# A dense expert table in another layout: 1152 column-major dense columns and 896 gathered ones, with the low parts shared between VectorE and GpSimd

## The chip, the cores and the metric

The kernel runs on one core of a Trainium2 chip. The metric is device time in microseconds from launch to end; lower is better. TensorE (PE in the profile), VectorE (DVE), ScalarE (ACT) and GpSimd (POOL) work side by side, each in the order in which its instructions were written; SyncE (SP) only issues DMAs, and GpSimd issues the indirect ones.

## What is computed

One decoder block on 256 tokens of width 2048: a mixing part (sparse attention and convolution), a layer norm that gives `y`, and then an expert-retrieval layer, which is where the change lies:

```python
q = (yb @ wq).reshape(bsz, PEER_BLOCK, PEER_HEADS, 2, PK_HALF)
...                                  # two top-16 lists per head, then the 16 best of 256 sums
eidx = jnp.take_along_axis(cidx, pos, axis=-1)
g = jax.nn.softmax(top.astype(jnp.float32), axis=-1)
u = u_tab[eidx]                      # u_tab: 16384 experts x 2048
v = v_tab[eidx]
h = jax.nn.gelu(jnp.einsum('btd,bthkd->bthk', yb, u))
return jnp.einsum('bthk,bthkd->btd', g * h, v).astype(y.dtype)
```

Each of the 256 tokens picks 16 experts in each of 8 heads, 128 experts in all, and needs the dot product of its own `y` with each picked row of `u_tab`. The numbers are float32, and matrix products are made exact enough by splitting each operand into a high and a low part and adding three products (high·high, high·low, low·high).

## The kernel before

The 2048 columns of `u_tab` are cut in two. For the first `UD` columns the products of **all** 16384 experts with all tokens are computed densely on TensorE. For the last `UG` columns only the picked rows are fetched, by indirect DMAs, and VectorE takes their dot products. A later stage picks the dense products of the chosen experts and adds the two.

The **dense stage** is the loop over `j` of 128 groups of 128 experts (`for j in range(P)` behind `later_steps`). Before the change a group is handled as two halves of 512 columns:

- `u_load` (SP) fetches 128 rows of 1024 columns into `ur`, `URB` groups ahead.
- `u_split` turns four blocks of 128x128 on TensorE into a PSUM tile `ut` (line 1235); ScalarE writes the high part `uh` from it (1238), VectorE the low part `ul` (1239).
- `u_mult` runs 12 matmuls of 128x256 for each half (`mm3`, lines 293 to 295), so 24 a group, summed in `hp`; `u_keep` (ScalarE, 1516) stores the sums in `W`.
- `dots_until` keeps the gathered side going. `gather` lets GpSimd issue one indirect DMA, one picked row for each of 128 tokens (1167); `dot` is VectorE's product and sum with the token's `y`, which lies in PSUM as `yp` (1178). There are 256 such gathers (2 token tiles of 128 picks). They go through a ring of `GBUFS` + `GMORE` = 5 buffers `gu`, so a gather waits on GpSimd until the dot that frees its buffer is done.
- `later_steps` gives VectorE a piece of the routing (top-16 search, expert numbers) in each round.

`LATE` gathers are left for the **lookup stage** behind the loop, which picks the dense products with small matmuls into `bank` tiles (1669, 1717); there a third of the products is done by GpSimd (`x_dot`, 1831) and summed by ScalarE (1841). A **value stage** with the second table follows (`f`, `gv`, `vr`, `vh`). Ahead of the loop the query product `pwq` runs, with low parts `lo` by GpSimd (254), and the first gathers and splits are mixed in. All orders are written out by hand; nothing is planned at run time.

Of the kernel before, what the change touches and what calls it, by code (L numbers as in the profile page):

```python
# [51 lines left out]
LATE = 52  # L52
# [8 lines left out]
UHB = 3  # L61
URB = 3
# [14 lines left out]
def tile_hybrid_block(  # L77
# [3 lines left out]
    w_out, ln1_g, ln1_b, wq, keys, u_tab, v_tab, ln2_g, ln2_b, out,  # L81
# [4 lines left out]
    u_tab, v_tab, out = u_tab[0], v_tab[0], out[0]  # L86
# [210 lines left out]
    def half_of(name, i):  # L297
        pool, n = ((slota, UK), (slots, KD - UK))[i]
        return flat3(pool.tile([P, n * T], F32R, name=f"{name}{n}", tag=f"t_{name[1]}"), n, T)

# [779 lines left out]
    def route_steps(h, tt, banked=False):  # L1080
# [32 lines left out]
        for s, dst in ((0, i1), (1, i2)):  # L1113
# [212 lines left out]
    def y_turn(cb, tt, low=True, tag="S"):  # L1326
        if yt[0][cb * 512 // UD] is None:
            yt[0][1], yt[1][1] = half_of("yh", 1), half_of("yl", 1)
# [5 lines left out]
        hs = chunks(yt[0], cb * 4, 4, ts)  # L1334
        nc.scalar.activation(hs, p3, AF.Copy)
        if low:
            nc.vector.tensor_tensor(chunks(yt[1], cb * 4, 4, ts), p3, hs.bitcast(F32), op=OP.subtract)
        else:
            return lambda: nc.vector.tensor_tensor(chunks(yt[1], cb * 4, 4, ts), p3, hs.bitcast(F32),
# [814 lines left out]
```

## Time and profile before

| what | value |
|---|---|
| time, median of 3 runs | 1638.65 us (1637.99 to 1642.5) |
| the profiled execution, its own time | 1637.97 us |
| its span, first to last instruction | 1636.2 us |
| TensorE busy | 1611.7 us, 99% of the span |
| VectorE busy | 1433.8 us, 88% |
| ScalarE, GpSimd busy | 811.0 us and 901.2 us |
| DMA | 475.19 MB, mean 290 GB/s |

Busy time is the time an engine had an instruction in work. Matmuls overlap each other, so the distance between the starts of two matmuls, and not their length, is what one costs. The DMA share is the mean busy share of the 16 DMA engines; GB/s is what they moved.

### The profile page before, as it was taken

How to read it: one execution, taken by the hardware profiler on the slowest of the kernel's cores; microseconds unless marked ns; L12 is line 12 of the kernel's file. 1: busy time of each engine (PE TensorE's matmuls, PEld its weight loads, DVE VectorE, ACT ScalarE, POOL GpSimd, SP SyncE). 2: the span in 40 equal slices, each digit the busy share in tenths (PEclk: the TensorE clock that was granted, in tenths of full speed). 3: DMA queues.
4: the chain of work that ended last, by engine and by line, in shares of the span. 5: the costliest groups of instructions: out<-in, count | busy, mean ns of one | idle time of the engine just before them, and what ended most of it. 6: DMA issues, size and time to landing. Idle time of an engine off the chain costs nothing.

```text
span 1636.2 us, 30621 instructions
## 1 busy us (share of the span) xinstructions
PE 1611.7 (99%) x11627; PEld 1495.9 (91%) x11627; DVE 1433.8 (88%) x2655; ACT 811.0 (50%) x1262; POOL 901.2 (55%) x661
## 2 busy tenths in 40 slices
PE   9999999999999999999999999999999999999997
PEld 9999999988999999999999997878888888888886
DVE  6999677756769999999999889988889999989998
ACT  5445766645434444444444445777444444444443
POOL 1886000065783333333333347757888887877883
PEclk9999999999999999999999999999999999999999
DMA  9774536365759999999999998776999999999997
GB/s 290 233 232 144 174 109 202 104 232 182 242 183 332 351 347 353 350 349 348 352 348 355 358 319 277 244 230 188 341 365 355 362 360 347 367 366 353 361 360 250
DMA packets 178348, 475.19 MB, mean 290 GB/s; under 512 B 18304, under 2 KB 86424, under 8 KB 177944
## 3 DMA queue, kind: packets, MB, share of 16 engines
q1 hardware_dynamic: 117188, 253.62, 45.7%
q0 software_dynamic: 57488, 218.66, 36.4%
q8 instruction: 91, 1.49, 0.4%
q10 hardware_dynamic: 3524, 0.95, 0.3%
q14 instruction: 57, 0.47, 0.1%
HBM read 468.32 MB, written 4.85 MB: 289 GB/s over the span
## 4 chain that ended last, share of the span: by engine, by line
PE 83%; DVE 7%; issue 3%; POOL 3%; ACT 2%; DMA 2%; POOLq 0%; DVEq 0%; ACTq 0%
PE f L294 9%; PE f L295 9%; PE f L293 9%; PE hp L295 7%; PE hp L293 7%; PE hp L294 6%; PE ut L1235 6%; PE bank L1717 2%; PE bank L1669 2%; DVE taps L487 2%; PE pwq L295 2%; PE pwq L294 2%; PE pwq L293 2%; DVE gu L1178 1%; PE mixa L293 1%
## 5 line engine op out<-in xcount | busy, mean ns | idle before, releaser
L1740 POOL DMA_INDIRECT gv<-in_peer_v_dram,e x256 | 396.6, 1549 | 98.1 <-DVE gacc L1745 52.5
L1167 POOL DMA_INDIRECT gu<-in_peer_u_dram,eu x206 | 193.2, 938 | 309.7 <-DVE gu L1178 219.3
L1780 ACT ACTIVATE vh<-vr 128x1408 fp32r<-128x1408 f32 (+1 forms) x129 | 175.7, 1364 | 275.0 <-DVE gacc L1745 233.0
L293 PE MATMUL hp<-yh,uh 128*128 128x256 f32 x1024 | 310.4, 303 | 0.4 <-ACT W L1516 0.3
L295 PE MATMUL hp<-yh,ul 128*128 128x256 f32 x1024 | 290.2, 283 | 0.9 <-DVE ul L1239 0.9
L294 PE MATMUL f<-vl,wh 128*128 128x512 f32 (+1 forms) x768 | 288.3, 375 | 1.5 <-DVE vl L1781 1.5
L294 PE MATMUL hp<-yl,uh 128*128 128x256 f32 x1024 | 289.2, 282 | 0.0
L293 PE MATMUL f<-vh,wh 128*128 128x512 f32 (+1 forms) x768 | 288.1, 375 | 0.0
L295 PE MATMUL f<-vh,wl 128*128 128x512 f32 (+1 forms) x768 | 287.7, 375 | 0.0
L1238 ACT ACTIVATE uh<-ut 128x512 fp32r<-128x512 f32 x256 | 152.7, 598 | 258.8 <-PE ut L1235 252.3
L254 POOL TENSOR_TENSOR lo<-raw,hi 128x1024 fp32r<-128x1024 f32 (+1 forms) x84 | 189.0, 2267 | 133.8 <-ACT hi L236 127.7
L1178 DVE SCALAR_TENSOR_TENSOR gu<-gu,yp 128x1024 f32<-128x1024 f32 x206 | 244.7, 1212 | 10.5 <-DMA gu<-in_peer_u_dram,eu 10.1
L1781 DVE TENSOR_TENSOR vl<-vr,vh 128x1408 fp32r<-128x1408 f32 (+1 forms) x129 | 206.4, 1601 | 40.0 <-ACT vh L1780 38.6
L1745 DVE SCALAR_TENSOR_TENSOR gacc<-gv,hv,gacc 128x640 f32<-128x640 f32 x247 | 207.6, 879 | 4.6 <-DMA gv<-in_peer_v_dram,e 4.3
L236 ACT ACTIVATE hi<-raw 128x1024 fp32r<-128x1024 f32 (+1 forms) x137 | 141.2, 1036 | 141.3 <-PE pcg L294 29.1
L295 PEld LDWEIGHTS hp<-yh,ul 128*128 128x128 f32 x1024 | 195.5, 191 | 1.5 <-DVE ul L1239 1.3
L293 PEld LDWEIGHTS hp<-yh,uh 128*128 128x128 f32 x1024 | 196.0, 191 | 0.8 <-ACT W L1516 0.8
L294 PEld LDWEIGHTS hp<-yl,uh 128*128 128x128 f32 x1024 | 196.5, 192 | 0.0
L1239 DVE TENSOR_TENSOR ul<-ut,uh 128x512 fp32r<-128x512 f32 x256 | 166.9, 681 | 18.4 <-ACT uh L1238 17.8
L294 PEld LDWEIGHTS f<-vl,wh 128*128 128x128 f32 x768 | 148.5, 193 | 23.8 <-DVE vl L1781 3.0
L293 PEld LDWEIGHTS f<-vh,wh 128*128 128x128 f32 x768 | 148.5, 193 | 20.8
L295 PEld LDWEIGHTS f<-vh,wl 128*128 128x128 f32 x768 | 148.7, 194 | 19.7
(409 smaller groups left out, 3506.1 us busy)
## 6 DMA issues: line engine op xcount, KB each, us to landing
vr<-in_peer_v_dram SPq DMA_DIRECT2D x128, 704.0 KB
ur<-in_peer_u_dram SPq DMA_DIRECT2D x128, 512.0 KB
raw<-in_w_in_dram SPq DMA_DIRECT2D x32, 1024.0 KB
raw<-in_w_out_dram SPq DMA_DIRECT2D x16, 1024.0 KB
raw<-in_peer_wq_dram SPq DMA_DIRECT2D x15, 1024.0 KB
gv<-in_peer_v_dram,e POOLq DMA_INDIRECT x256, 7.4
gu<-in_peer_u_dram,eu POOLq DMA_INDIRECT x206, 7.7
raw<-in_w_in_dram SPq DMA_DIRECT2D x4, 608.0 KB
```

Of the source, the lines that this page charges most:

```text
L254: e.tensor_tensor(lo[:, a:b], src[:, a:b], hi[:, a:b].bitcast(F32), op=OP.subtract)
L293: nc.tensor.matmul(acc, lhsT=ah, rhs=bh, start=start, stop=False)
L294: nc.tensor.matmul(acc, lhsT=ah, rhs=bl, start=False, stop=False)
L295: nc.tensor.matmul(acc, lhsT=al, rhs=bh, start=False, stop=stop)
L1167: nc.gpsimd.indirect_dma_start(out=gt, out_offset=None, in_=ug, in_offset=bass.IndirectOffsetOnAxis(ap=fl(eu, tt)[:, c:c + 1], axis=0))
L1178: nc.vector.scalar_tensor_tensor(gt, gt, 1.0, yr, op0=OP.mult, op1=OP.mult, accum_out=hv[:, tt, c:c + 1])
L1238: nc.scalar.activation(uh, pt, AF.Copy)
L1239: nc.vector.tensor_tensor(ul, pt, uh.bitcast(F32), op=OP.subtract)
L1740: nc.gpsimd.indirect_dma_start(out=gvs[j, tt], out_offset=None, in_=v_tab, in_offset=bass.IndirectOffsetOnAxis(ap=fl(e4, tt)[:, j:j + 1], ...
L1745: engine.scalar_tensor_tensor(gacc[:, tt], gvs.pop((j, tt)), wv[:, tt, j:j + 1], gacc[:, tt], op0=OP.mult, op1=OP.add)
L1780: nc.scalar.activation(vh, src[:, s], AF.Copy)
L1781: (nc.gpsimd if early else nc.vector).tensor_tensor(vl, src[:, s], vh.bitcast(F32), op=OP.subtract)
```

## The change

The dense part grows from 1024 to 1152 columns (9 blocks of 128 instead of 8), and the gathered part shrinks from 1024 to 896. Both parts are now two arrays of their own, laid out ahead of the launch: `u_dense` holds each group's 128 rows already turned, block by block, in the form in which TensorE takes its stationary operand, and `u_rows` holds the 896 gathered columns of each expert in a row of its own. The second index table `eu` falls away, since `e4` now indexes both tables.

A group is split whole: ScalarE writes `uh` (1152 columns) from `ur`, ScalarE copies 768 columns of `ur` into a PSUM tile `ut`, VectorE subtracts those 768, and GpSimd subtracts the other 384 in SBUF. `u_mult` runs all 18 products with `uh` first and the 9 with `ul` last. The split of group `j + 2` stands behind `u_mult(j)` instead of between its halves. Buffers: `uh` and `ul` 2 (of 1152 columns) instead of 3 (of 512), `ur` 4 instead of 3. `LATE` goes from 52 to 58. The activations `y` keep their cut at column 1024 where they are computed, and are cut at 1152 where `yh` and `yl` are turned (`y_turn`).

```diff
-UG = 1024
+UG = 896
 UD = D - UG
 UK = UD // P
+HC = D // 2
+HK = HC // P
+UV = 6 * P
-LATE = 52
+LATE = 58
-UHB = 3
-URB = 3
+UHB = 2
+URB = 4
...
-        nc.vector.tensor_scalar(eu[:, tt, h], ef, float(D // UG), float(D // UG - 1),
-                                op0=OP.mult, op1=OP.add)
...
-            out=gt, out_offset=None, in_=ug,
-            in_offset=bass.IndirectOffsetOnAxis(ap=fl(eu, tt)[:, c:c + 1], axis=0))
+            out=gt, out_offset=None, in_=u_rows,
+            in_offset=bass.IndirectOffsetOnAxis(ap=fl(e4, tt)[:, c:c + 1], axis=0))
...
-        nc.sync.dma_start(uraw[j], u_tab[j * P:(j + 1) * P, :UD])
+        nc.sync.dma_start(uraw[j], u_dense[j * P:(j + 1) * P])
...
-    def u_split(n, early=False):
-        j, b = divmod(n, NP)
+    def u_split(j, early=False):
         raw = uraw[j]
-        pt = psb.tile([P, 512], F32, name=f"ut{j}_{b}", tag="ToT"[n], bufs=1) if early else psu.tile([P, 512], F32, name=f"ut{j}_{b}", tag="ut", bufs=4)
-        for i in range(4):
-            k = b * 4 + i
-            nc.tensor.transpose(pt[:, i * P:(i + 1) * P], raw[:, k * P:(k + 1) * P], ident)
-        uh = pu.tile([P, 512], F32R, name=f"uh{j}_{b}", tag="uh", bufs=UHB)
-        ul = pu.tile([P, 512], F32R, name=f"ul{j}_{b}", tag="ul", bufs=UHB)
-        nc.scalar.activation(uh, pt, AF.Copy)
-        nc.vector.tensor_tensor(ul, pt, uh.bitcast(F32), op=OP.subtract)
+        uh = pu.tile([P, UD], F32R, name=f"uh{j}", tag="uh", bufs=UHB)
+        ul = pu.tile([P, UD], F32R, name=f"ul{j}", tag="ul", bufs=UHB)
+        nc.scalar.activation(uh, raw, AF.Copy)
+        src = raw[:, :UV]
+        if not early:
+            src = psu.tile([P, UV], F32, name=f"ut{j}", tag="ut", bufs=2)
+            nc.scalar.activation(src, raw[:, :UV], AF.Copy)
+        nc.vector.tensor_tensor(ul[:, :UV], src, uh[:, :UV].bitcast(F32), op=OP.subtract)
+        nc.gpsimd.tensor_tensor(ul[:, UV:], raw[:, UV:], uh[:, UV:].bitcast(F32), op=OP.subtract)
...
+        for k in range(UK):
+            s = slice(k * P, k * P + P)
+            nc.tensor.matmul(hps[j], lhsT=uh[:, s], rhs=chunk(yh, k), start=k == 0, stop=False)
+            nc.tensor.matmul(hps[j], lhsT=uh[:, s], rhs=chunk(yl, k), start=False, stop=False)
+        for k in range(UK):
+            s = slice(k * P, k * P + P)
+            nc.tensor.matmul(hps[j], lhsT=ul[:, s], rhs=chunk(yh, k), start=False, stop=k == UK - 1)
...
             if j + URB < P:
                 u_load(j + URB)
-            for n in range(j * NP, j * NP + NP):
-                if 2 < n + 2 < P * NP:
-                    u_split(n + 2)
-                u_mult(n)
-            dots_until(min(upto, routed, issued + CATCH), ending)
+            u_mult(j)
             if j:
                 u_keep(j - 1)
+            if j + 2 < P:
+                u_split(j + 2)
+            dots_until(min(upto, routed, issued + CATCH), ending)
...
+    u = inputs["peer_u"][0]
+    inputs["peer_u_dense"] = u[:, :UD].reshape(P, P, UK, P).transpose(0, 3, 2, 1).reshape(P * P, UD)
+    inputs["peer_u_rows"] = u[:, UD:]
```

TensorE, one half of a group in the dense loop before (`ut` is the turned block of a later half, `hp` the sum of the group; numbers are buffer names):

```order
L1235 MATMUL ut_0_6220<-ident,ur_6108 128x128 x4
L293 MATMUL hp_6229<-yh_4531,uh_0_6169 128x256
L294 MATMUL hp_6229<-yl_4532,uh_0_6169 128x256
L295 MATMUL hp_6229<-yh_4531,ul_0_6170 128x256
...
L1235 MATMUL ut_1_6242<-ident,ur_6108 128x128 x4
```

TensorE, the end of one group and the start of the next in the same loop now:

```order
L1515 MATMUL hp_6089<-yh_4530,uh_6025 128x256
L1516 MATMUL hp_6089<-yl_4531,uh_6025 128x256
L1519 MATMUL hp_6089<-yh_4530,ul_6026 128x256 x9
L1515 MATMUL hp_6135<-yh_4530,uh_6071 128x256
L1516 MATMUL hp_6135<-yl_4531,uh_6071 128x256
```

The two blocks of four transposes a group are gone, nine pairs with `uh` and then nine matmuls with `ul` stand in a group, and nothing else stands between groups.

VectorE, about one group in the middle of the loop before (dots are the 1178 rows, the rest belongs to the routing):

```order
L1239 TENSOR_TENSOR ul_0_7529<-ut_0_7523,uh_0_7528 128x512
L1239 TENSOR_TENSOR ul_1_7551<-ut_1_7545,uh_1_7550 128x512
L1178 SCALAR_TENSOR_TENSOR gu_51_7352,hv<-gu_51_7352,yp 128x1024
L1178 SCALAR_TENSOR_TENSOR gu_52_7405,hv<-gu_52_7405,yp 128x1024
L1104 MAX top<-scr_7518 128x8
```

VectorE, about one group at such a place now:

```order
L1237 TENSOR_TENSOR ul_7776<-ut_7778,uh_7775 128x768
L1179 SCALAR_TENSOR_TENSOR gu_64_7602,hv<-gu_64_7602,yp 128x896
L1179 SCALAR_TENSOR_TENSOR gu_65_7646,hv<-gu_65_7646,yp 128x896
L1119 TENSOR_TENSOR oh_7788<-fab_7697,iota 128x256
L1122 TENSOR_TENSOR oh_7788<-oh_7788,vf_4323 128x256
```

One subtraction of 768 stands where two of 512 stood, and each dot is 896 wide.

GpSimd, in the loop before, where it only issues gathers:

```order
L1167 DMA gu_49_7296<-in_peer_u_dram,eu 128x1024
L1167 DMA gu_50_7349<-in_peer_u_dram,eu 128x1024
L1167 DMA gu_51_7352<-in_peer_u_dram,eu 128x1024
L1167 DMA gu_52_7405<-in_peer_u_dram,eu 128x1024
L1167 DMA gu_53_7458<-in_peer_u_dram,eu 128x1024
```

GpSimd, in the loop now:

```order
L1168 DMA gu_57_7371<-in_peer_u_rows_dram,e_4315 128x896
L1238 TENSOR_TENSOR ul_7412<-ur_7286,uh_7411 128x384
L1168 DMA gu_58_7419<-in_peer_u_rows_dram,e_4315 128x896
L1238 TENSOR_TENSOR ul_7455<-ur_7329,uh_7454 128x384
L1168 DMA gu_59_7462<-in_peer_u_rows_dram,e_4315 128x896
```

A subtraction of 384 columns now stands in GpSimd's queue once a group, and the gathers behind it wait for it.

## Rows read from the trace of the kernel before

**Rows 1.** The page: the chain that ended last, share by engine.

```profile
PE 83%; DVE 7%; issue 3%; POOL 3%; ACT 2%; DMA 2%; POOLq 0%; DVEq 0%; ACTq 0%
```

**Rows 2.** Windows: query product's end, dense stage, lookup stage; columns as headed.

```profile
core 0: us, PE busy (x) PEld busy (x) DVE busy (x) ACT busy (x) POOL busy (x), PEclk, DMA share, GB/s
394.00:487.90 93.90, 92.10 (x768) 91.26 (x767) 64.88 (x291) 34.47 (x47) 76.65 (x41) 1.00 0.70 229
487.90:970.00 482.10, 480.86 (x4092) 479.07 (x4092) 460.74 (x987) 222.73 (x392) 178.74 (x192) 1.00 0.95 346
970.00:1090.00 120.00, 115.13 (x943) 94.66 (x942) 106.51 (x180) 82.94 (x160) 89.00 (x72) 0.99 0.78 255
```

**Rows 3.** Timeline of TensorE, 701.5 to 703.7 us: start, length (us), instruction.

```profile
701.59 0.28 PE L295 MATMUL hp<-yh,ul 128*128 128x256 f32 x1
701.71 0.60 PE L1235 MATMUL ut<-ident,ur 128*128 128x128 f32 x4
702.07 0.36 PE L293 MATMUL hp<-yh,uh 128*128 128x256 f32 x1
702.27 0.28 PE L294 MATMUL hp<-yl,uh 128*128 128x256 f32 x1
...
703.47 0.28 PE L295 MATMUL hp<-yh,ul 128*128 128x256 f32 x1
```

**Rows 4.** Groups by line on VectorE, 500 to 900 us: busy us, mean ns | idle.

```profile
L1178 DVE SCALAR_TENSOR_TENSOR gu<-gu,yp 128x1024 f32<-128x1024 f32 x160 | 189.9, 1211 | 0.2 <-ACT yp L1491 0.2
L1239 DVE TENSOR_TENSOR ul<-ut,uh 128x512 fp32r<-128x512 f32 x212 | 137.4, 681 | 3.7 <-ACT uh L1238 3.3
```

**Rows 5.** Timeline of VectorE, 604 to 607.5 us.

```profile
603.38 1.28 DVE L1239 TENSOR_TENSOR ul<-ut,uh 128x512 fp32r<-128x512 f32 x2
604.58 1.21 DVE L1178 SCALAR_TENSOR_TENSOR gu<-gu,yp 128x1024 f32<-128x1024 f32 x1
...
605.72 1.21 DVE L1178 SCALAR_TENSOR_TENSOR gu<-gu,yp 128x1024 f32<-128x1024 f32 x1
```

**Rows 6.** Window of most of the dense stage, columns as in rows 2.

```profile
494.00:900.00 406.00, 404.86 (x3451) 404.06 (x3450) 397.71 (x872) 187.28 (x326) 151.34 (x162) 1.00 0.95 349
```

**Rows 7.** Gathers in the dense stage: windows of `gu` alone (busy, count).

```profile
486.00:970.00 484.00, 228.26 (x383) 177.94 (x190) 1.00 0.95 346
```

**Rows 8.** Short windows at full DMA share, and the value stage; columns as in rows 2.

```profile
610.00:615.00 5.00, 5.00 (x46) 5.00 (x44) 4.90 (x14) 2.60 (x5) 1.87 (x2) 1.00 1.00 367
625.00:630.00 5.00, 5.00 (x45) 5.00 (x44) 4.90 (x14) 2.63 (x5) 2.29 (x3) 1.00 1.00 383
432.00:436.00 4.00, 4.00 (x36) 4.00 (x35) 4.00 (x28) 1.54 (x2) 4.00 (x2) 1.00 1.03 419
1300.00:1500.00 200.00, 200.00 (x939) 174.92 (x939) 180.98 (x181) 86.70 (x78) 160.55 (x103) 1.00 0.98 360
```

**Rows 9.** Groups by line on ScalarE, whole span: busy us, mean ns | idle.

```profile
L1780 ACT ACTIVATE vh<-vr 128x1408 fp32r<-128x1408 f32 x126 | 174.2, 1382 | 272.6 <-DVE gacc L1745 233.0 <-PE f L295 32.1 <-DVE vl L1781 4.0
L1516 ACT ACTIVATE W<-hp 128x256 f32<-128x256 f32 x128 | 81.3, 635 | 2.8 <-PE hp L295 2.8
```

**Rows 10.** Timeline of GpSimd in the lookup stage, 992 to 999 us.

```profile
992.88 0.94 POOL L1167 DMA_INDIRECT spare<-in_peer_u_dram,eu  x1 [0.30 <-DVE spare L1178]
994.13 0.94 POOL L1167 DMA_INDIRECT morel<-in_peer_u_dram,eu  x1 [0.30 <-issue]
995.09 2.38 POOL L1831 TENSOR_TENSOR spare<-spare,morel 128x1024 f32<-128x1024 f32 x1
```

**Rows 11.** Timeline of GpSimd ahead of the query product, 355 to 366 us.

```profile
355.79 1.29 POOL L254 TENSOR_TENSOR lo<-raw,hi 128x512 fp32r<-128x512 f32 x1 [0.70 <-ACT hi L236]
...
363.94 1.79 POOL L254 TENSOR_TENSOR lo<-raw,hi 128x512 fp32r<-128x512 f32 x1 [0.93 <-ACT hi L236]
```

**Rows 12.** The gathers of 500 to 900 us: issue to landing.

```profile
DMA to landing us min/median/max: 6.3/7.8/9.8
```

**Rows 13.** Waits of 494 to 900 us: who for whom, total us, times, longest.

```profile
POOL gu L1167 <- DVE gu L1178: 183.0, 90, 5.4
```

More of the change, by code (lines that the diff above doesn't have):

```diff
@@ L80, in tile_hybrid_block @@
     x, w_in, pos_k, w1_k, w2_k, pos_v, w1_v, w2_v, dw_w, dw_b, cln_g, cln_b,
-    w_out, ln1_g, ln1_b, wq, keys, u_tab, v_tab, ln2_g, ln2_b, out,
+    w_out, ln1_g, ln1_b, wq, keys, u_dense, u_rows, v_tab, ln2_g, ln2_b, out,
     dbg=None, stop=None,
@@ L85, in tile_hybrid_block @@
     x, w_in, w_out, wq = x[0], w_in[0], w_out[0], wq[0]
-    u_tab, v_tab, out = u_tab[0], v_tab[0], out[0]
+    v_tab, out = v_tab[0], out[0]
     dbg = dbg or {}
@@ L295, in mm3, with half_of @@
         nc.tensor.matmul(acc, lhsT=al, rhs=bh, start=False, stop=stop)
-    def half_of(name, i):
-        pool, n = ((slota, UK), (slots, KD - UK))[i]
-        return flat3(pool.tile([P, n * T], F32R, name=f"{name}{n}", tag=f"t_{name[1]}"), n, T)
+    def half_of(name, i, k0):
+        pool, most = ((slota, UK), (slots, HK))[i]
+        n = (k0, KD - k0)[i]
+        return flat3(pool.tile([P, most * T], F32R, name=f"{name}{i}", tag=f"t_{name[1]}"), n, T)
     def halves(name):
-        return [flat3(pool.tile([P, n * T], F32R, name=f"{name}{n}", tag=f"t_{name[1]}"), n, T)
-                for pool, n in ((slota, UK), (slots, KD - UK))]
+        return [half_of(name, i, HK) for i in range(2)]
     def chunk(t, k, s=slice(None)):
-        return t[0][:, k, s] if k < UK else t[1][:, k - UK, s]
+        k0 = t[0].shape[1]
+        return t[0][:, k, s] if k < k0 else t[1][:, k - k0, s]
     def chunks(t, k, n, s):
-        return t[0][:, k:k + n, s] if k < UK else t[1][:, k - UK:k - UK + n, s]
+        k0 = t[0].shape[1]
+        return t[0][:, k:k + n, s] if k < k0 else t[1][:, k - k0:k - k0 + n, s]
     def add_cols(w, c0, t, name, dve, done):
@@ L1291, in y_part @@
     def y_part(cb, tt):
-        return part[0][:, cb, tt] if cb * 512 < UD else yg[:, tt, cb * 512 - UD:cb * 512 - UD + 512]
+        return part[0][:, cb, tt] if cb < 2 else yg[:, tt, cb * 512 - HC:cb * 512 - HC + 512]
     def y_center(cb, tt):
@@ L1333, in y_turn, with lows @@
         p3 = flat3(pt, 4, P)
[L1334 to L1335 removed]
+        at = min(max(UK - cb * 4, 0), 4)
+        spans = [(a, e) for a, e in ((0, at), (at, 4)) if e > a]
+        for a, e in spans:
+            nc.scalar.activation(chunks(yt[0], cb * 4 + a, e - a, ts), p3[:, a:e], AF.Copy)
+        def lows():
+            for a, e in spans:
+                hs, ls = (chunks(t, cb * 4 + a, e - a, ts) for t in yt)
+                nc.vector.tensor_tensor(ls, p3[:, a:e], hs.bitcast(F32), op=OP.subtract)
         if low:
[L1337 removed]
+            lows()
         else:
[L1339 to L1340 removed]
+            return lows
     if True:
@@ L1348, in tile_hybrid_block @@
         force("early", "early")
-        yt.extend([half_of(name, 0), None] for name in ("yh", "yl"))
+        yt.extend([half_of(name, 0, UK), None] for name in ("yh", "yl"))
         i = nphase + 6
```

38 lines of the change are left out of this document (14 added, 24 removed).

## The prediction

> **What bounds the kernel now.** I read the chain that ended last first, then windows by stage, then the timelines of the engines inside the stage that the change touches. The chain is 83% TensorE [rows 1], so a change pays where TensorE works without gaps and gets less to do. The dense stage, 482.1 us long, is such a place: TensorE is busy for 480.9 of them [rows 2]. But three resources are nearly full there at once. VectorE is busy for 397.7 of 406.0 us and the DMA engines for a share of 0.95 [rows 6]. So the question is not whether TensorE gets less to do, but which of the others stops it next.
>
> What a matmul costs is read from starts: from 702.27 to 703.47 us ten steps take 1.20 us, 0.12 each, and from the start of a block of four transposes (701.71) to the second matmul behind it (702.27) are 0.56 us, so the block costs 0.44 [rows 3]. A group is 24 matmuls and two blocks: 24 x 0.12 + 2 x 0.443 = 3.77 us, and 128 x 3.77 is the stage. Nothing hides the transposes: the matmuls on both sides follow without a gap.
>
> **TensorE's part of the change.** The two blocks go (0.89 us a group), three matmuls come (0.36): 27 x 0.12 = 3.24 us a group, 415 us for 128. Were TensorE alone, the stage would shrink by 67 us. That is the floor of the sum. The new order inside a group (all `uh`, then `ul`) costs nothing by itself, as each matmul loads its own weights before and after, and it gives the low part 18 matmuls (2.2 us) more time.
>
> **DMA.** Before, 193 gathers of 128 rows of 4 KB fall into the stage (256 - 52 + 2 = 206 stand before or in the loop, 13 of them ahead of it; the window from 486 us on counts 190 [rows 7]), and 125 loads of 512 KB. That is 166.7 MB, and 346 GB/s over 482.1 us [rows 2] is 166.8 MB, so the count holds. After: 187 gathers of 128 x 3584 B (85.8 MB) and 124 loads of 589,824 B (73.1 MB), 158.9 MB. To finish in 415 us the DMA engines would have to move 383 GB/s. What can they do? Three bounds. The stage's own 349 GB/s at a share of 0.95 makes 367 at a full share [rows 6]. Five-microsecond windows at full share show 367 to 383 (two of six in this stage are shown), and the value stage, with rows of other lengths, holds 360 for 200 us at 0.98 [rows 8]. For 4 us ahead of the stage, with several plain loads queued, 419 were moved [rows 8]. So 360 is proven for long stretches, 383 for short ones with this mix. I take 367: 158.9 MB / 367 GB/s = 433 us, 49 less than now; the ends are 360 (441 us) and 383 (415 us, where TensorE binds).
>
> The Trainium skill, HBM Reference, section Specifications, gives a core about 358 GB/s as its share of the memory, and adds that a core streaming alone measures well above it, near 425. By 358 the stage would take an estimated 444 us and the kernel about 1601; by 425 TensorE would bind. The 419 GB/s above agree with the second figure for 4 us, and no run here yet shows it for longer.
>
> **VectorE.** Its busy time is 397.7 us for 107.8 groups, 3.69 a group [rows 6]. Two subtractions of 512 take 1.20 us from start to start of what follows, and a dot 1.14 [rows 5]. One subtraction of 768, by proportion, takes 0.90; a dot of 896 takes 1.00. There were 160 dots in 106.2 groups [rows 4], 1.51 each, and there will be 187/128 = 1.46. So 3.69 - 0.30 - (1.51 x 1.14 - 1.46 x 1.00) = 3.13 us. If a dot did not shrink at all it would be 3.33. VectorE fits under 433/128 = 3.38 either way, and fits under 3.24 only if dots shrink.
>
> **ScalarE.** It gets `uh` of 1152 and the copy of 768; from 1408 columns in 1.382 us [rows 9] proportion gives 1.13 and 0.75, with `W` at 0.635 [rows 9] 2.52 us a group. If both cost the full 1.382 it is 3.40, just the DMA figure. The high part waits for the 18th matmul of group j, the copy ends some 0.9 us behind the group's end, and the low part is wanted 3.24 + 2.16 = 5.4 us behind it, so a split has over 3 us to spare.
>
> **GpSimd.** A new kind of work in its queue: one subtraction of 384. Two-input operations took 1.29 us at 512 columns [rows 11] and 2.38 at 1024 [rows 10]; the line through both gives 1.02 at 384. Gathers follow each other at 1.25 us (992.88 to 994.13) [rows 10], 1.46 x 1.25 = 1.83 a group. Sum 2.85 us. Some subtractions of 512 took 1.79 [rows 11]; at that price the sum is 3.62 us and GpSimd would bind at 463 us. I take 1.02. Behind the subtraction wait the gathers, and for these the dots five gathers later.
>
> The Trainium skill, SBUF — State Buffer, section Who interferes with whom, says that a VectorE instruction with two SBUF inputs and a GpSimd instruction that reads SBUF keep each other out for a whole instruction, while one with a single SBUF input does not contend. The steady loop's large VectorE operations have one operand in PSUM, so by that rule only the small routing operations could hold GpSimd up. The 1.29 and 1.79 us above are compatible with that rule but do not prove it.
>
> **The ring of gathers.** Five buffers at 1.46 a group last 3.42 groups, 11.1 us at 3.24 and 11.6 at 3.38. In them fit a dot (1.0), the landing (median 7.8 us, longest 9.8 [rows 12]), and the wait in GpSimd's queue, at most one subtraction and one more gather, 2.3 us: 11.1 with the median. Before, the wait was none: GpSimd sat idle for 183.0 us until dots were done [rows 13]. So the ring is just wide enough; this and the DMA rate push the same way, and are why I don't go below 433.
>
> **What lies around the stage.** Three blocks of transposes go ahead of it (3 x 0.44); the fourth buffer adds 0.79 MB to the early loads, 2.1 us of DMA time where the share is 0.70 [rows 2], four pieces ahead of need: -1 us, between -1.3 and +2. The split `y_turn` and the dropped index operation lie under matmuls; without that cover they cost or give some 0.5 us. The lookup stage gets six gathers more (56 for 50): GpSimd +7.5 us for these and +1.5 for products, 89.0 to 98 of 120 us [rows 2], VectorE 2 us less. TensorE idles 4.9 us there; I take +2 between 0 and +9. The value stage is untouched.
>
> **Sum.** -49 - 1 + 2 = -48 us. Against the profiled execution's own 1637.97 us that is 1590; the median of the runs is 0.7 higher, which changes nothing. The measurement can tell some 0.3%, 5 us, from no change.
>
> **Rivals.**
> - *DMA binds* (forecast, 0.48): 355 to 375 GB/s, 424 to 448 us, the kernel at 1581 to 1605. For it: the three rates above. About 0.1 of this chance is a rate held near 358, the first figure of the page.
> - *TensorE stays the bound* (0.20): 415 to 424 us, 1571 to 1581. For it: 383 and 419 GB/s in short windows, and longer rows in the dense loads. Against it: no long stretch over 360, and VectorE at 3.13 of 3.24.
> - *GpSimd or a lower rate takes most of it* (0.20): a subtraction at 1.79 us gives 463 us and 1620; an unchanged 346 GB/s gives 459 us and 1616. For it: both prices occur in the trace. Against: 1.29 us where nothing disturbs. By the page's rule the routing operations would be the cause, about half this chance.
> - *No change* (0.04): the new wait just eats the gain, 1633 to 1643.
> - *Slower* (0.08): the ring of five decides. If landings go to 9.8 us and each gather waits the full 2.3 us on GpSimd, a turn takes 13.1 us, 3.83 a group, 490 us: 1647. It decides from landing plus wait of 11.9 us on (3.77 x 3.42 - 1.0). For it: the ring has no slack at 3.24 us, and GpSimd issues in order. Against: landings now have a median of 7.8, and VectorE waits 0.2 us in total for dots [rows 4], so the data now lies there before its turn.
>
> The range 1570 to 1620 holds all of the first two and about 0.6 of the third, 0.80 in all. Faster by over 0.3%: 0.88; within: 0.04; slower: 0.08.
>
> **What would show it.** In the changed profile the stage from the first to the last `hp` should last 433 us (415 to 463) at about 367 GB/s and a DMA share of 0.98 or more; TensorE should show idle time before matmuls with `ul` that ends with VectorE or GpSimd, and VectorE idle before `gu` dots that ends with the DMA. If TensorE has no gaps, the second rival is right. If GpSimd is busy nearly throughout with subtractions well over 1.0 us, the third. Wrong altogether would be matmuls at more than 0.12 us from start to start, which no row suggests.

## The result: 1589.5 us, and the profile after

The changed kernel takes 1589.5 us (median of four runs, 1585.8 to 1594.2) against 1638.3 us for the kernel before on the same chip (four runs): a ratio of 0.9702 [0.9682, 0.9723]. The forecast was 1590. The profiled execution took 1588.2 us, its span is 1586.4 us.

The total agrees to half a microsecond, but two of its terms do not. The dense stage, from its first `hp` matmul to the lookup stage's first, went from 481.5 to 424.5 us: 57 gained where 49 were forecast. The lookup stage, from there to the value product's first matmul, went from 159.8 to 168.3 us: 8.5 lost where 2 were forecast. (In [rows 2] the border lies at the round 970.00 us, 0.6 us behind the end of the dense stage.) Windows of the changed kernel by stage, with the same columns as [rows 2]: the dense stage, its steady part, its end, and the lookup stage:

```profile
core 0: us, PE busy (x) PEld busy (x) DVE busy (x) ACT busy (x) POOL busy (x), PEclk, DMA share, GB/s
486.90:911.40 424.50, 417.79 (x3461) 416.69 (x3459) 392.75 (x832) 310.10 (x391) 309.70 (x312) 1.00 0.99 374
494.00:850.00 356.00, 354.75 (x2955) 354.43 (x2954) 344.80 (x747) 266.07 (x330) 266.29 (x270) 1.00 1.00 387
850.00:911.40 61.40, 55.94 (x449) 55.17 (x447) 45.28 (x82) 39.22 (x51) 38.75 (x40) 0.97 0.92 315
911.40:1079.70 168.30, 158.89 (x1284) 131.30 (x1284) 139.37 (x240) 118.29 (x226) 124.08 (x105) 0.96 0.71 227
```

The second row decides the forecast's main question. Over 356 us TensorE is busy for all but 1.25, while the DMA engines move 387 GB/s, 20 above the 367 that the sum took as their limit. 2955 matmuls are 109.4 groups, so a group takes 3.25 us; the floor was 3.24. TensorE falls idle mainly in the third row, the last 61 us. Its gaps there, from the timeline of TensorE between 850 and 873 us, are 5.5 us long together:

```profile
853.59 0.39 PE L1515 MATMUL hp<-yh,uh 128*128 128x256 f32 x1 [1.85 <-ACT W L1522]
866.12 0.39 PE L1515 MATMUL hp<-yh,uh 128*128 128x256 f32 x1 [1.08 <-ACT W L1522]
872.27 0.33 PE L1562 MATMUL colsg<-ident,gs 128*128 128x128 f32 x1 [2.54 <-DVE gs L1142]
```

The prices inside the steady part, as groups of VectorE, GpSimd and ScalarE between 500 and 800 us (busy us, mean ns, then the idle time ahead):

```profile
L1179 DVE SCALAR_TENSOR_TENSOR gu<-gu,yp 128x896 f32<-128x896 f32 x135 | 142.4, 1080 | 0.0
L1237 DVE TENSOR_TENSOR ul<-ut,uh 128x768 fp32r<-128x768 f32 x92 | 87.4, 950 | 3.4 <-ACT ut L1236 2.1 <-issue 0.7
L1168 POOL DMA_INDIRECT gu<-in_peer_u_rows_dram,e x134 | 129.7, 968 | 71.7 <-DVE gu L1179 45.7 <-issue 3.9 <-DVE pab L1113 3.4
L1238 POOL TENSOR_TENSOR ul<-ur,uh 128x384 fp32r<-128x384 f32 x93 | 95.7, 1029 | 1.9
L1232 ACT ACTIVATE uh<-ur 128x1152 fp32r<-128x1152 f32 x93 | 108.7, 1169 | 74.1 <-issue 59.0 <-PE hp L1516 7.3 <-POOL ul L1238 6.8
L1236 ACT ACTIVATE ut<-ur 128x768 f32<-128x768 f32 x93 | 74.0, 796 | 0.0
```

GpSimd's subtraction has a mean of 1.03 us (forecast 1.02). VectorE is busy for 344.80 us in 109.4 groups, 3.15 a group (forecast 3.13), 0.1 us less than TensorE needs. VectorE's dots wait 0.0 us for data, so the ring of five gathers does not run dry.

### The profile page after: what moved, and what is told of

It is laid out like the page before. It is cut to its first block, busy times and chain, and to the rows that moved or that the text cites. A ratio compares the mean times of both kernels' runs of the same rounds, so it can differ in the third digit from the quotient of the medians.

```text
span 1586.4 us, 29450 instructions
## 1 busy us (share of the span) xinstructions
PE 1550.8 (98%) x10987; PEld 1435.9 (91%) x10987; DVE 1367.0 (86%) x2509; ACT 899.4 (57%) x1266; POOL 1044.3 (66%) x791
## 4 chain that ended last, share of the span: by engine, by line
PE 83%; DVE 7%; DMA 3%; POOL 3%; issue 2%; ACT 2%; POOLq 0%; ACTq 0%; DVEq 0%
PE f L297 10%; PE f L298 10%; PE f L296 10%; PE hp L1515 8%; PE hp L1516 8%; PE hp L1519 7%; PE bank L1722 3%; DVE taps L492 2%; PE pwq L298 2%; PE pwq L297 2%; PE pwq L296 2%; PE bank L1674 2%; DMA feat<-fr 1%; PE mixa L296 1%; PE pcg L297 1%
## 5 line engine op out<-in xcount | busy, mean ns | idle before, releaser
L1515 PE MATMUL hp<-yh,uh 128*128 128x256 f32 x1152 | 283.8, 285 | 4.2 <-ACT W L1522 4.2
L1516 PE MATMUL hp<-yl,uh 128*128 128x256 f32 x1152 | 283.4, 284 | 0.0
L1168 POOL DMA_INDIRECT gu<-in_peer_u_rows_dram,e x200 | 193.6, 968 | 117.9 <-DVE gu L1179 72.0
L1515 PEld LDWEIGHTS hp<-yh,uh 128*128 128x128 f32 x1152 | 222.5, 193 | 4.8 <-ACT W L1522 4.8
L1516 PEld LDWEIGHTS hp<-yl,uh 128*128 128x128 f32 x1152 | 222.6, 193 | 0.0
L1179 DVE SCALAR_TENSOR_TENSOR gu<-gu,yp 128x896 f32<-128x896 f32 x200 | 211.2, 1080 | 12.2 <-DMA gu<-in_peer_u_rows_dram,e 12.2
L1232 ACT ACTIVATE uh<-ur 128x1152 fp32r<-128x1152 f32 x128 | 149.6, 1168 | 95.6 <-issue 69.3
L1519 PE MATMUL hp<-yh,ul 128*128 128x256 f32 x1152 | 159.3, 284 | 0.0
L1519 PEld LDWEIGHTS hp<-yh,ul 128*128 128x128 f32 x1152 | 147.6, 192 | 0.1
L1237 DVE TENSOR_TENSOR ul<-ut,uh 128x768 fp32r<-128x768 f32 x126 | 119.9, 952 | 26.1 <-ACT ut L1236 23.2
```

Source lines behind the costliest of these rows:

```text
L1168: nc.gpsimd.indirect_dma_start(out=gt, out_offset=None, in_=u_rows, in_offset=bass.IndirectOffsetOnAxis(ap=fl(e4, tt)[:, c:c + 1], axis=0))
L1179: nc.vector.scalar_tensor_tensor(gt, gt, 1.0, yr, op0=OP.mult, op1=OP.mult, accum_out=hv[:, tt, c:c + 1])
L1515: nc.tensor.matmul(hps[j], lhsT=uh[:, s], rhs=chunk(yh, k), start=k == 0, stop=False)
L1516: nc.tensor.matmul(hps[j], lhsT=uh[:, s], rhs=chunk(yl, k), start=False, stop=False)
L1519: nc.tensor.matmul(hps[j], lhsT=ul[:, s], rhs=chunk(yh, k), start=False, stop=k == UK - 1)
```

## The experiments

Twelve kernels were run. Each ratio is to the kernel before on the same chip, with its 95% interval; the chips differ (the kernel before took 1638 to 1645 us on them), so ratios compare and medians do not. "Stage" and "lookup" are the dense and the lookup stage in us, with the borders named above, each from the one profiled execution.

| kernel | ratio [interval] | stage | lookup |
|---|---|---|---|
| before | 1 | 481.5 | 159.8 |
| changed | 0.9702 [0.9682, 0.9723] | 424.5 | 168.3 |
| dense rows padded to 8 KB | 0.9699 [0.9676, 0.9722] | 423.2 | 168.2 |
| gathers of 4096 bytes | 0.9773 [0.9750, 0.9796] | 437.0 | 168.5 |
| 1024 dense columns | 0.9747 [0.9724, 0.9771] | 427.1 | 181.7 |
| low part from SBUF, two engines | 1.0048 [1.0034, 1.0063] | 483.2 | 170.5 |
| low part from SBUF, VectorE alone | 0.9860 [0.9841, 0.9879] | 454.3 | 168.5 |
| 52 late gathers | 0.9630 [0.9614, 0.9646] | 424.5 | 154.8 |
| 46 late gathers | 0.9648 [0.9628, 0.9668] | 427.7 | 163.8 |
| fewer products on GpSimd | 0.9656 [0.9637, 0.9675] | 425.4 | 166.4 |
| one product moved | 0.9684 [0.9669, 0.9699] | 425.0 | 168.8 |
| feature stores by SyncE | 0.9694 [0.9677, 0.9710] | 426.1 | 168.7 |
| 52 late, stores a step later | 0.9630 [0.9615, 0.9646] | 426.7 | 160.0 |
| 52 late, eight buffers | 0.9616 [0.9600, 0.9632] | 424.3 | 153.7 |

### What the DMA engines can carry

First question: why 387 GB/s, where the sum took 367? One theory was that the new table's contiguous blocks help.

```diff
-        nc.sync.dma_start(uraw[j], u_dense[j * P:(j + 1) * P])
+        nc.sync.dma_start(uraw[j], u_dense[j * P:(j + 1) * P, :UD])
+    inputs["peer_u_dense"] = _np.pad(inputs["peer_u_dense"], ((0, 0), (0, D - UD)))
```

> The turned dense table lies in rows of 8 KB of which 4.6 KB are read, as the old table was; bytes, packets and order stay. Theory A (the DMA engines got faster because each dense load is now one contiguous block): the dense queue falls back to some 350 GB/s for a full share, 367 together, the dense stage becomes DMA bound and takes some 433 us instead of 424, the kernel some 1598. Theory B (faster because two gathered rows of 3584 bytes now go in one packet): the stage stays at 424 us and the dense queue at 385 GB/s for a full share. Theory C (there never was a limit near 367, the earlier rate was only what TensorE asked for): also 424.

The padded table gave the same rate and the same time, so contiguity is not it. Window of 494 to 850 us with it:

```profile
494.00:850.00 356.00, 354.75 (x2955) 354.46 (x2954) 344.93 (x747) 266.18 (x330) 267.01 (x270) 1.00 1.01 387
```

The second kernel gathers 1024 columns and uses 896, which adds 12.3 MB to the stage:

```diff
-ga.tile([P, UG], F32, name=f"gu{tt}_{c}", tag="gu")
+ga.tile([P, HC], F32, name=f"gu{tt}_{c}", tag="gu")
+        gt = gt[:, :UG]
-    inputs["peer_u_rows"] = u[:, UD:]
+    inputs["peer_u_rows"] = _np.concatenate([u[:, UD:], u[:, HC:UD]], 1)
```

> The gathers of the dense stage fetch rows of 4096 bytes (896 used columns and 128 unused) where 3584 were fetched; dots stay 896 wide. Bytes of the stage rise from 158.9 to 171.2 MB, 415 GB/s at the pace of TensorE. Theory B (paired packets made the rate): one packet for each row again, the gather queue falls from 390 to 376 GB/s for a full share, the stage is DMA bound at 370 to 380 GB/s and takes 450 to 463 us, the kernel 1615 to 1628. Theory A (contiguous dense loads made it): a rate near 395 is kept, 433 us, 1598. Theory C (no limit below 415): 424 us, 1589.

Window of 500 to 800 us:

```profile
500.00:800.00 300.00, 293.00 (x2416) 291.42 (x2415) 283.92 (x623) 217.97 (x272) 214.92 (x220) 0.99 1.01 402
```

The gathers' queue in the same window (packets, MB, share of the engines' time):

```profile
q0 software_dynamic: 18714, 68.33, 57.5%
```

TensorE's largest gap, from its timeline, and VectorE's wait for landings in the window (us in total, times, longest):

```profile
759.38 0.98 PE L1520 MATMUL hp<-yh,ul 128*128 128x256 f32 x6 [4.07 <-DVE ul L1238]
DVE gu L1180 <- DMA gu<-in_peer_u_rows_dram,e: 12.2, 20, 1.6
```

At 402 GB/s over 300 us TensorE has 7.0 us of gaps in the window (13.7 in the stage). VectorE's dots wait 12.2 us for landings, where none waited in the changed kernel, and the median landing takes 9.4 us in place of 6.5. So this is about where transfers begin to hold the engines up, with this mix of gathers and loads, and the forecast's 367 was no limit. The 349 GB/s of [rows 6] were what a TensorE that was busy for 404.86 of 406 us asked for; dividing them by a busy share of 0.95 does not give what the engines can move. The same queue of the changed kernel, same window, shows how the rows were packed:

```profile
q0 software_dynamic: 10757, 61.64, 52.6%
```

10,757 packets of 5.7 KB carry the 3584-byte rows, where rows of 4096 bytes went at 3.7 KB a packet. The unpaired rows still moved at 402 GB/s, so the packing did not make the rate either. Of the padded kernel's three theories C is left: there was no limit near 367. The Trainium skill, HBM Reference, section Specifications, gives about 358 GB/s as a core's share and about 425 for a core alone. By the share the stage would have lasted an estimated 444 us; the trace agrees with the second figure in that it shows 387 and 402 with gathers in the mix, but no run here reaches 425.

### Which part of the change pays

```diff
-UG = 896
+UG = 1024
```

> 1024 dense and 1024 gathered columns, as the kernel before had, but in the new column-wise layout without transposes. TensorE's floor is 24 x 0.1195 x 128 = 367 us. Theory A (with TensorE relieved, VectorE binds: 3.08 us a group now, and 0.15 to 0.18 more for longer dots, 3.25 a group): dense stage 412 to 420 us, TensorE with 45 us or more of gaps that end with VectorE; the shift of 128 columns then gained nothing, and the removal of the transposes all. Theory B (DMA binds: 163 MB at 402 GB/s): 405 us, gaps of TensorE and VectorE both ending with DMA. Theory C (the unpaired rows of 4096 bytes land later, as when 1024 columns were gathered and 896 used, and the ring of five runs dry): 430 us or longer, and the column shift is worth over 5 us. Lookup stage 168 plus 1 to 6 us for 56 longer gathers.

Window of 494 to 850 us:

```profile
494.00:850.00 356.00, 326.60 (x2563) 314.77 (x2563) 351.51 (x732) 247.50 (x323) 226.02 (x262) 0.99 1.00 385
```

2563 matmuls are 106.8 groups of 24, 3.33 us each, where 24 x 0.12 = 2.9 would do. VectorE is busy for 351.51 of 356 us, 3.29 a group. So without the shift of 128 columns VectorE binds (theory A; its 3.25 a group was 0.08 low, hence 427 us and not 412 to 420, and TensorE's gaps in the stage are 36 us and not 45). The rest of the change gives 54 of the 57 us in the stage: the transposes are gone, and GpSimd takes a part of each subtraction from VectorE. No kernel that drops only the transposes was run, so the two are not told apart here. The column shift gives 3 us in the stage, and the lookup stage, whose gathers, dots and products are longer with 1024 columns, is 13 us shorter with it.

### Where VectorE reads

In the change VectorE takes its 768 columns from PSUM, where ScalarE has copied them. This kernel saves the copy and reads SBUF:

```diff
         src = raw[:, :UV]
-        if not early:
-            src = psu.tile([P, UV], F32, name=f"ut{j}", tag="ut", bufs=2)
-            nc.scalar.activation(src, raw[:, :UV], AF.Copy)
```

> Only the source of VectorE's 768-column low part changes: it reads the raw columns in SBUF instead of ScalarE's copy in PSUM, and the copy (0.80 us a group on ScalarE) goes. Theory (two SBUF inputs on VectorE keep GpSimd's SBUF-reading subtraction out, as the Trainium skill says, SBUF - State Buffer, Who interferes with whom): GpSimd's subtraction of 384 columns grows from a mean of 1.03 us to 1.8 or more, GpSimd from 2.4 to some 3.3 us a group, and the dense stage from 424 to 430 us or longer. Rival (no interference that matters): the subtraction stays at 1.03 to 1.1 us, the stage at 423 to 425, the kernel at 1586 to 1590 us.

It is the largest effect of all: 483.2 us for the stage, and the kernel is 0.5% slower than before. The rival missed altogether. The theory's interference came, but not its victim: in the steady part it is VectorE that pays, not GpSimd. Window of 494 to 850 us:

```profile
494.00:850.00 356.00, 325.17 (x2544) 309.45 (x2543) 352.57 (x649) 164.13 (x191) 236.79 (x231) 1.00 0.94 331
```

The groups of both engines' subtractions in that window:

```profile
L1234 DVE TENSOR_TENSOR ul<-ur,uh 128x768 fp32r<-128x768 f32 x94 | 146.0, 1553 | 0.7 <-ACT uh L1232 0.7
L1235 POOL TENSOR_TENSOR ul<-ur,uh 128x384 fp32r<-128x384 f32 x94 | 96.8, 1030 | 1.9
```

And both engines' timelines from 519 to 533 us (start, length), the subtractions alone:

```profile
519.97 2.32 DVE L1234 TENSOR_TENSOR ul<-ur,uh 128x768 fp32r<-128x768 f32 x1
525.02 0.94 DVE L1234 TENSOR_TENSOR ul<-ur,uh 128x768 fp32r<-128x768 f32 x1
527.77 0.95 DVE L1234 TENSOR_TENSOR ul<-ur,uh 128x768 fp32r<-128x768 f32 x1
530.49 2.34 DVE L1234 TENSOR_TENSOR ul<-ur,uh 128x768 fp32r<-128x768 f32 x1
...
520.45 1.02 POOL L1235 TENSOR_TENSOR ul<-ur,uh 128x384 fp32r<-128x384 f32 x1
525.79 1.05 POOL L1235 TENSOR_TENSOR ul<-ur,uh 128x384 fp32r<-128x384 f32 x1
528.70 1.04 POOL L1235 TENSOR_TENSOR ul<-ur,uh 128x384 fp32r<-128x384 f32 x1
530.98 1.02 POOL L1235 TENSOR_TENSOR ul<-ur,uh 128x384 fp32r<-128x384 f32 x1
```

VectorE's subtraction has two lengths. Of 107 between 495 and 905 us, 59 took 0.95 us on average and overlapped one of GpSimd's by at most 0.25 us; 48 took 2.27 us, and each of them spans a whole subtraction of GpSimd (overlap 1.00 to 1.04 us). GpSimd's 107 in that time stay at 1.00 to 1.13 us. VectorE thus needs 352.57/94 = 3.75 us a group and binds.

The ends tell more than the lengths. In all 48 meetings VectorE ends 0.82 to 0.83 us behind GpSimd, although its record starts anywhere from 0.08 to 0.67 us ahead: nearly all of its 0.95 us of work comes after GpSimd is done. That is why the stretch (1.3 us) can be longer than GpSimd's whole instruction. Outside that window the roles are also the other way round. Nine of GpSimd's 128 subtractions in the whole stage, two at its start and seven from 908 us on, took 1.77 to 1.80 us. Each of them starts 0.05 us behind one on VectorE that keeps its 0.96 us, and ends 0.87 to 0.89 us behind it:

```profile
908.78 0.96 DVE L1234 TENSOR_TENSOR ul<-ur,uh 128x768 fp32r<-128x768 f32 x1 [0.99 <-issue]
908.82 1.78 POOL L1235 TENSOR_TENSOR ul<-ur,uh 128x384 fp32r<-128x384 f32 x1
```

If this is a mutual exclusion, then taking GpSimd's help away must make the kernel faster:

```diff
-        nc.vector.tensor_tensor(ul[:, :UV], src, uh[:, :UV].bitcast(F32), op=OP.subtract)
-        nc.gpsimd.tensor_tensor(ul[:, UV:], raw[:, UV:], uh[:, UV:].bitcast(F32), op=OP.subtract)
+        nc.vector.tensor_tensor(ul, raw, uh.bitcast(F32), op=OP.subtract)
```

> VectorE makes the whole low part, 1152 columns, from SBUF; GpSimd makes none of it and the copy to PSUM goes. Theory (VectorE with two SBUF inputs and GpSimd's tensor operation exclude each other, which stretched 48 of 107 subtractions from 0.95 to 2.27 us when both worked from SBUF): with GpSimd left only with gathers, no subtraction is stretched; each takes 1.38 to 1.42 us, VectorE 3.5 us a group, the dense stage 452 to 460 us, the ratio to before 0.985 to 0.992, so VectorE with more work makes a faster kernel than the 1.0048 with GpSimd's help. Rival (two SBUF inputs are slow now and then by themselves, from the DMA's writes or the gathers' descriptors): a part of the subtractions stays stretched to over 2.3 us, the stage lasts 480 us or longer, the ratio is 1.00 or above.

Group of VectorE's subtraction, 494 to 850 us:

```profile
L1233 DVE TENSOR_TENSOR ul<-ur,uh 128x1152 fp32r<-128x1152 f32 x101 | 136.4, 1351 | 1.0 <-ACT uh L1232 1.0
```

It did: 454.3 us and 0.986. The 1152 columns take 1.35 us on average and none in that window takes over 1.43. Of all 128 one was stretched, ahead of the stage, and it met the last of GpSimd's subtractions for the query product (`lo`), the second of two in this row:

```profile
478.20 3.39 DVE L1233 TENSOR_TENSOR ul<-ur,uh 128x1152 fp32r<-128x1152 f32 x1
475.64 4.73 POOL L257 TENSOR_TENSOR lo<-raw,hi 128x1024 fp32r<-128x1024 f32 x2
```

So two SBUF inputs alone are not slow; the meeting with GpSimd is. The Trainium skill, SBUF — State Buffer, section Who interferes with whom, states this as an exclusive lock between a VectorE instruction with two SBUF inputs and a GpSimd one that reads SBUF, and says that one with a single SBUF input does not contend. The trace agrees with both halves: 2.27 us against 0.95 with two, and 0.95 us on VectorE beside 1.03 on GpSimd in the changed kernel. By the page the order of issue decides who waits. The trace agrees in the nine cases, where VectorE's record starts first and GpSimd waits. In the 48 VectorE's record starts first too, and VectorE waits, so the starts of the records do not tell who waits.

### What six more late gathers cost

The changed kernel leaves 56 gathers for the lookup stage, six more than before; its constant for it is 58, and 52 takes them back:

```diff
-LATE = 58
+LATE = 52
```

> LATE back to 52: six gathers and dots move from the lookup stage into the dense loop. If the lookup stage grew from 159 to 168 us because of these six, it comes back to 159 to 161, the dense stage stays at 424 (VectorE has 0.14 us a group to spare for 0.05 dots), and the kernel takes 1580 to 1582. If it grew for another reason (clock, late first gathers, wider tables) it stays at 168 and the kernel at 1589.

Windows of that kernel, dense and lookup stage:

```profile
486.90:911.40 424.50, 419.19 (x3462) 418.15 (x3463) 396.55 (x844) 309.79 (x391) 315.88 (x318) 0.99 0.99 381
911.40:1066.10 154.70, 151.69 (x1284) 126.18 (x1284) 133.56 (x232) 115.94 (x222) 114.19 (x97) 1.00 0.72 228
```

The dense stage takes the six gathers for nothing, and the lookup stage is 13.6 us shorter, 5 us below that of the kernel before. Against the changed kernel's row, TensorE is busy for 7.2 us less, with a granted clock of 1.00 in place of 0.96, and idle for 6.4 less. Six more the same way:

```diff
-LATE = 58
+LATE = 46
```

> 46 late gathers in place of 58. Lookup stage: with 52 it has 1.9 us of TensorE gaps left, so 46 can give at most 2 us more there: 152 to 154 us. Dense stage: 199 gathers and 124 loads, 164.4 MB, 396 GB/s over 415 us. Theory A (DMA carries 402 GB/s): stage 424 to 427 us, kernel 1575 to 1578 us. Theory B (VectorE, 3.08 us a group and 0.1 more for dots, or the ring of five, binds): stage 428 to 440 us with gaps of TensorE that end with VectorE, kernel 1579 to 1592 us.

The stage lasted 427.7 us with 394 GB/s between 500 and 800 us, at the upper end of theory A or just past it, while the lookup stage grew to 163.8 us with new gaps and a clock of 0.97. Half of those gaps is one of 4.38 us, ahead of 1034.63 us, for which the profile shows no cause; without it the stage would still be longer than with 52. The intervals of 52 and 46 overlap, so no gain was found below 52, and the lookup stage does not follow the number of late gathers in a straight line.

Why does it lose with 58? One row stands out. VectorE's product of the gates took 2.22 us, and GpSimd had begun a product in SBUF 0.03 us ahead of it: the same meeting as above. TensorE's transpose then waits 2.42 us (timelines of VectorE, GpSimd and TensorE):

```profile
959.07 2.22 DVE L1693 TENSOR_TENSOR gs<-top,i 128x128 f32<-128x128 f32 x1 [1.04 <-ACT top L1689]
959.04 2.09 POOL L1836 TENSOR_TENSOR moreh<-moreh,morel 128x896 f32<-128x896 f32 x1
963.97 0.47 PE L1653 MATMUL bank<-ident,gs 128*128 128x128 f32 x1 [2.42 <-DVE top L1678]
```

In the window just behind it the granted clock is 0.58, near the lower of the engine's two levels (1.2 of 2.4 GHz):

```profile
965.00:971.00 6.00, 5.84 (x32) 4.74 (x32) 3.00 (x6) 2.67 (x5) 3.04 (x2) 0.58 0.60 210
```

One kernel moves just that product to VectorE:

```diff
-        if i % 3 == XPOOL and i0 <= i < 2 * P - 4:
+        if i % 3 == XPOOL and i != 217 and i0 <= i < 2 * P - 4:
```

> The changed kernel with 58 late gathers, but one product of the lookup stage, the one that GpSimd began at 959.04 us just as VectorE began the product of the gates (959.07 us, 2.22 us long in place of some 0.3 to 0.5), is a dot on VectorE. Theory (that one meeting of two SBUF readers delays VectorE by 1.7 us, TensorE's transpose at 961.55 waits 2.42 us for it, and the granted clock falls to about half behind it): the gates' product takes 0.3 to 0.5 us, the gap shrinks to 1.0 us or less, the clock stays at 1.00 in the 6 us behind it, the lookup stage goes from 168.4 to 162 to 165 us, the ratio from 0.970 to 0.966 to 0.968. Rival (VectorE comes late there by its dots, which wait for landings, and one more dot makes it worse): a gap of 1.5 us or more stays, the lookup stage lasts 166 to 170 us, the ratio is 0.969 to 0.972.

Timelines of VectorE and TensorE at the same step:

```profile
960.89 0.29 DVE L1693 TENSOR_TENSOR gs<-top,i 128x128 f32<-128x128 f32 x1 [1.03 <-ACT top L1689]
963.86 0.33 PE L1653 MATMUL bank<-ident,gs 128*128 128x128 f32 x1 [0.49 <-DVE top L1678]
```

And the window behind it:

```profile
965.00:971.00 6.00, 5.95 (x52) 5.03 (x52) 5.97 (x11) 3.54 (x8) 3.35 (x3) 1.00 0.63 213
```

At its place the theory holds: 0.29 us, a gap of 0.49, the clock at 1.00. But the lookup stage lasts 168.8 us as before, with gaps elsewhere (1.35 us at 926, 1.35 at 980, 1.50 at 1004), and the ratio lies between the two expectations; its interval overlaps that of the changed kernel. So this one meeting explains the gap and the clock behind it, not the longer stage. The other kernel halves GpSimd's products:

```diff
-        if i % 3 == XPOOL and i0 <= i < 2 * P - 4:
+        if i % 6 == XPOOL and i0 <= i < 2 * P - 4:
```

> 58 late gathers as in the changed kernel; of the products in the lookup stage GpSimd takes every sixth instead of every third, VectorE the others as dots. Theory A (GpSimd's queue, three gathers and a product of 2.09 us by turns, lets the gathers land late, and VectorE waits in order at the dots, 12.6 us for DMA against 5.2 with 52 late gathers; and products stretch VectorE's operations with two SBUF inputs): VectorE's waits for DMA fall to 4 to 7 us, the lookup stage from 168 to 155 to 161 us, the ratio from 0.970 to 0.962 to 0.966, though VectorE gets 9 or 10 dots more (10 us). Theory B (the number of dots on VectorE, or the DMA itself, costs): the lookup stage stays at 166 us or grows to 175, the ratio is 0.969 to 0.975.

VectorE's dots on the `spare` and `moreh` buffers no longer wait for landings: 4.3 and 3.5 us in the changed kernel, none here (the first dots, on `gu`, keep 5.2). The ratio falls to 0.9656, inside theory A's band; the profiled run, its slowest (1587.6 us, the others 1581.7 to 1584.4), shows a stage of 166.4 us, in which the gates' product again met one on GpSimd (2.11 us), the transpose waited 2.08 us and the clock then was 0.50 for 6 us. So the waits for landings and the meeting occur, and each can be removed. Neither kernel gives back the whole 14 us, and both removed together with 58 late gathers was not tried. This kernel has both fewer waits and fewer products on GpSimd that can meet VectorE, so which of the two gave its gain is not shown, and what makes up the 14 us stays partly open.

### The gaps at the stage's end

Three kernels aimed at the 5.5 us from 850 us on, where ScalarE's `W` stands behind the feature stores in its queue. First the stores go to SyncE's queue:

```diff
-                    nc.scalar.dma_start(feats[n][:, r].rearrange("a p c -> p a c"), fr)
+                    nc.sync.dma_start(feats[n][:, r].rearrange("a p c -> p a c"), fr)
```

> The ten stores of the routing features are issued by SyncE and not by ScalarE. If the stall of TensorE at 850 to 885 us (5.5 us of idle time) comes from ScalarE's queue, which waits in order for VectorE before each of these stores while the splits stand behind them, most of it goes: dense stage 419 to 421 us, kernel 1584 to 1586. If it comes from VectorE's own work there (features, softmax of the gates, the transposes that wait for it), it stays: 424 and 1589.

No gain: now the dense loads stand behind the stores on SyncE, ScalarE's split waits 5.49 us for such a load, and TensorE waits 3.64 us at 848 us. Then, with 52 late gathers, ScalarE issues each store one step later, and the gate transposes come one step later:

```diff
+                for hn, hr, ht in held:
+                    nc.scalar.dma_start(feats[hn][:, hr].rearrange("a p c -> p a c"), ht)
+                held = [(n, r, fr) for r in ((0, 1) if f == 0 else (f + 1,))]
...
+        yield
```

> 52 late gathers in place of 58, and in the last 20 groups each feature store is issued by ScalarE one group later, and the gate transposes one group later. Theory (TensorE's 4.8 to 5.5 us of gaps from 850 us on come from ScalarE and TensorE waiting in order for VectorE's small operations, which queue behind dots): the gaps at 851, 865 and 870 us go, the dense stage ends at 907 to 908 us in place of 911.9, and the kernel takes 1572 to 1574 us against 1577.1 with 52 late gathers alone. Rival (the lag of VectorE is longer than a group, or the drain of the steps at the end takes the stall): stage unchanged at 424 to 426 us and 1576 to 1578 us.

The gaps at `W` are 3.77 and 2.99 us long, where 52 late gathers alone have 3.00 and 1.79. The gap at the transposes is gone, but it is gone with 52 late gathers alone too. VectorE's row suggests a cause, a feature row that waits until a store has landed and so frees its buffer:

```profile
857.18 0.29 DVE L1546 TENSOR_SCALAR fr<-i 128x256 bf16<-128x256 f32 x1 [3.43 <-DMA feat<-fr]
```

So eight buffers (both users of the tag), at the old place of the stores:

```diff
-name=f"fr{n}{f}", tag="scr", bufs=4)
+name=f"fr{n}{f}", tag="scr", bufs=8)
```

> 52 late gathers, and eight instead of four buffers for the feature rows that VectorE writes and ScalarE's queue stores (the same instructions in the same order). Theory (from 850 us on the rows of the second feature wait for a buffer until the store of the first has landed, VectorE waits for that in order, ScalarE's store for VectorE, and W and TensorE behind it): the gaps at 851 and 865 us shrink from 4.8 to under 2 us, the dense stage from 424.5 to 420 to 422 us, the ratio to before from 0.963 to 0.960 to 0.9615. Rival (VectorE is late by its own queue of dots, or the stores wait for room beside the gathers): gaps of 4 us or more stay and the ratio stays at 0.9625 to 0.9640.

VectorE's wait is gone, but the gaps stay (2.27, 0.47, 2.26 and 1.53 us): ScalarE's `W` still waits 3.7 us at its own stores, until a store has landed. The ratio of 0.9616 is the lowest measured, but its interval overlaps that of 52 late gathers alone. All three aims missed; what a store in ScalarE's queue waits for there stays open.

## Why the forecast was right, and where its steps were not

The forecast of 1590 us was met, but by luck: the mechanism that it named as the likeliest did not come, and two terms were wrong in opposite directions.

- **TensorE's part** held: 3.25 us a group against a floor of 3.24, matmuls 0.12 apart.
- **DMA binds at 367 GB/s** was the step that failed. The rate was demand, not capacity: 387 GB/s were moved in the steady part and 402 in an experiment. Of the signs that the forecast named, the DMA share of 0.98 or more came (1.00), but not the waits: no dot waited for a landing in the steady part, and TensorE had 1.25 us of gaps in 356. The second rival (TensorE stays the bound, chance 0.20) is what the steady part shows; with the 5.5 us at the end the stage came to 424.5 us, just above that rival's range of 415 to 424. The kernel's 1589.5 us lie in the range of the rival that failed (1581 to 1605) and not in that of the one that came (1571 to 1581), because the lookup stage lost what the dense stage gained beyond the forecast.
- **VectorE, ScalarE and GpSimd** were priced within 0.05 us an instruction, and VectorE's group within 0.02. The third rival's 1.79 us came once, for the first of 128 subtractions, at 487.11 us, when VectorE still read SBUF; the others stay at 1.01 to 1.05. In the steady part VectorE's subtraction has one operand in PSUM, and the experiments show that this keeps it at 0.95 us, where two operands in SBUF took 2.27 in 48 of 107 cases. It carries the gain: without it the kernel is slower than before.
- **The ring of five** had its slack: no dot waited in the steady part, with landings at a median of 6.5 us.
- **Around the stage**, -1 us ahead of it held. The lookup stage was mis-sized: +8.5 us, near the upper end of its range of 0 to +9, not +2. Counting the gathers' issue time on GpSimd left out VectorE's waits for their landings in order (12.6 us against 4.2 before) and the granted clock (0.96 against 0.99). The change's own step from 52 to 58 late gathers made the kernel slower: 0.9702 against 0.9630.
- So the sum came out by two errors of opposite sign: 8 us too little gain forecast in one stage and 6.5 us too little loss in another.

## What to carry to other kernels

A transfer rate seen while another engine is the bound is that engine's demand; it says nothing of what the queues can carry, and neither does the rate over the busy share. When VectorE and GpSimd work side by side, look at where the operands lie: one operand of VectorE in PSUM may be worth a ScalarE copy, and a helper that VectorE has to wait for can cost more than it takes over. When work is moved from a full stage to one with idle time, follow the waits in order there, not the busy time.

## What the runs showed of the hardware

- Side by side with GpSimd's 1.03 us subtraction, VectorE's subtraction of 768 columns from SBUF took 2.27 us in 48 of 107 cases and 0.95 in the others; VectorE then ended 0.82 to 0.83 us behind GpSimd. In nine other meetings GpSimd's took 1.77 to 1.80 us and VectorE's 0.96.
- Gathered rows of 3584 bytes went at 5.7 KB a packet, rows of 4096 bytes at 3.7 KB.
- The DMA engines held 402 GB/s for 300 us with gathers and loads mixed.
- In the lookup stage gaps of 2.08 and 2.42 us on TensorE were followed by some 6 us at a granted clock of 0.50 and 0.58; with the gap at 0.49 us (one product moved) the clock stayed at 1.00. But the length of the gap does not decide it alone: in the changed kernel's dense stage the clock was 0.72 from 853 to 859 us, behind a gap of 1.85 us, and 1.00 behind the longest gap, 2.54 us up to 872.27 us:

```profile
872.00:879.00 7.00, 6.73 (x56) 6.73 (x57) 4.38 (x8) 5.67 (x8) 3.27 (x4) 1.00 0.87 279
```
